# Replicated rows for the 32x32 block inverses: one transfer per block and half, and X with its chunks outside

## The chip, the cores and the metric

The kernel runs on one core of a Trainium2 chip. A core has five engines, each with its own instruction stream in a fixed order: PE (TensorE, matrix products; its weight load is listed as PEld), DVE (VectorE), ACT (ScalarE), POOL (GpSimd) and SP (SyncE), which here does nothing but issue DMA transfers. Sixteen DMA engines move the data. Engines wait for each other, and for transfers, by semaphores. The metric is the device time of one execution in microseconds (us); less is better.

## The reference, cut to what matters

Two layers over 2048 tokens of width 1024. The first is a gated DeltaNet (GDN, 8 heads), the second gated linear attention (GLA, 4 heads); each has an input projection, a mixer over chunks of tokens, a gate, an output projection and a layer norm. The change touches GDN alone, where each chunk needs a unit lower triangular system solved:

```python
kb = k * beta
A = jnp.where(strict, jnp.einsum('bhncd,bhnsd->bhncs', kb, k) * decay, 0.0)
eye = jnp.eye(CHUNK, dtype=A.dtype)
rhs = jnp.concatenate([v * beta, kb * jnp.exp(gc)[..., None]], axis=-1)
uw = lax.linalg.triangular_solve(A + eye, rhs, left_side=True, lower=True, unit_diagonal=True)
```

The kernel forms the inverse of A + eye explicitly, for chunks of 128 tokens.

## The kernel before

**Tiling.** Tokens go in 4 groups of 512, each 4 chunks (NC) of 128. A *unit* is one head of one layer in one group: 32 GDN units and 16 GLA units, 48 in all, in the order of PHASES: GDN groups 0 and 1, GLA group 0, GDN group 2, GLA 1, GDN 3, GLA 2, GLA 3. GDN units thus come as numbers 0 to 31 among themselves; "unit 12" below is head 4 of group 1. Each unit has four parts: gemms (input projections on PE, products written to PSUM tiles psg), preps (per-chunk matrices), chains (the recurrence over 4 chunks, PSUM tiles psh), outs (output projection, psc and pso).

**Weights.** Projection weights stream from HBM through 9 buffers called wc, 256 KB per load (wc<-wk), issued by SP as soon as a buffer is free; output weights (wo) come by the same queue. On their first use weights come as wraw and are split by ACT and POOL into a high and a low part, which are stored as wk.

**Inverse of the 32x32 blocks** (in gdn_prep, lines 845 to 865). D1 holds the matrix A of 4 chunks, 128x128 each. ACT copies the four diagonal 32x32 blocks into a tile X0 (named own in the code) of 128 partitions x (32 columns x 4 chunks). Two stores on ACT's queue bring it to DRAM: whole rows as blk (late in the code), the first 16 columns as blkq (early). Then SP loads the tile Arep back, in which every partition of block b holds a copy of the block's rows: rows 16 to 31 in full from blk (Arep<-blk, 1 MB), rows 0 to 15 cut to 16 columns from blkq (Arep<-blkq, 0.5 MB). The inverse X starts from the identity (a POOL copy) and is found in 31 steps, q from 31 down to 1, each two DVE operations: Xt = (row q of Arep) × (column q of X), then X −= Xt. Steps 31 to 16 read the first part of Arep, steps 15 to 1 the second. DVE then spreads X into the block-diagonal Tm, transposes it to U, and PE joins the blocks to 64 and 128.

**Layout.** X is (column j, chunk n) with the chunk innermost: a step works on q·4 adjacent elements.

**Order.** No order is written by hand. A recorder notes every operation; a planner (place) then simulates the engines with a cost per operation and a lag until its result can be read, and fixes each engine's order. For a DMA the cost is the time on SP's queue and the lag the time until it has landed. Engines run that order whatever really happens: an engine that waits holds up all that stands behind it. An Arep transfer waits on SP for its store, and the wc and wo loads stand behind it.

Of the kernel before, what the change touches and what calls it, by code (L numbers as in the profile page):

```python
# [12 lines left out]
ALU = mybir.AluOpType  # L13
# [3 lines left out]
P = 128  # L17
# [5 lines left out]
NC = TG // P  # L23
# [90 lines left out]
def size_of(shape):  # L114
    n = 1
    for k in shape[1:]:
        n *= k
    return n


class Recorder:
# [61 lines left out]
    def cost(self, op, dst, every):  # L183
        key = op.key
        n = size_of(dst.shape)
        psum = any(isinstance(a, View) and a.of.psum for a in every)
        op.func = None
        if key == "t":
            mov = size_of(every[2].shape) if op.name == "matmul" else size_of(every[1].shape)
            if op.name == "transpose":  # L190
                op.cost = 2 * dst.shape[0] / 2.4 + 4
            elif every[1].dtype == F32:
                op.cost = 2 * max(mov / 1.2 + 3, 0.85 * every[1].shape[-1] + 2)
            else:
                op.cost = mov / 2.25 + 4.5
            op.lag = 210
            op.func = op.name == "matmul" and min(dst.shape[0], every[1].shape[0]) < P
        elif key == "d":
            size = 4 * n * dst.shape[0]
            tag = dst.of.tag if isinstance(dst, View) else ""  # L200
            op.cost, op.lag = 630 if tag == "wc" or tag[:2] == "wk" else 560 if tag == "wraw" else 480, DMA_LAG + size / 170
            if tag == "Arep":
                op.cost, op.lag = 720, REP_LAG + size / 400
            elif tag in ("y", "woraw"):
                op.lag = 9500
        elif key == "a":
            size = 4 * n * dst.shape[0]
            op.cost, op.lag = 340, DMA_LAG + size / 170 + (2500 if isinstance(every[1], View) and every[1].of.tag == "xraw" else 0)
        elif key == "v":
            n = max(n, max(size_of(a.shape) for a in every))  # L210
            took = (150 if psum else 160) + 1.04 * n
            if op.name in ("tensor_reduce", "copy_predicated", "tensor_tensor_scan"):
                took += 1.0 * n
            if op.name != "tensor_tensor" and any(isinstance(a, (View, bass.AP)) and size_of(a.shape) == 1
                                                  for a in every[1:]):
                took += 62 if psum or n < 512 else 85
            op.cost, op.lag = took - 80, 80 + LAG
        elif key == "s":
            took = (165 if psum else 210) + 0.833 * n
            if any(isinstance(op.kw.get(k), (View, bass.AP)) for k in ("scale", "bias")):  # L220
                took += 100 + 67 * ("scale" in op.kw and "bias" in op.kw)
            if "accum_out" in op.kw:
                took += 190
            if op.name == "activation":
                op.func = "ln" if op.args[2] == AF.Ln else None if op.args[2] in (AF.Copy, AF.Square, AF.Identity,
                                                                                 AF.Abs) else "exp"
            op.cost, op.lag = took - 95, 95 + LAG
        else:
            took = 140 + 2.8 * n if len(every) > 2 else 185 + n
            if op.args[-1] == ALU.pow:  # L230
                took = 450 + 160 * n
            op.cost, op.lag = took - 40, 40 + LAG
# [143 lines left out]


LAG, DRAIN = 60, 35
DMA_LAG, REP_LAG, SLACK = 3500, 8500, 100
INSPECT = None  # L380


# [1 line left out]
def trunk(ctx, tc, x, xT, w_in1, conv, a_log, dt_bias, nw1, w_out1, w_in2, gk_up, gk_b, nw2, w_out2,  # L384
# [3 lines left out]
    v, s, g = (rec.engine(e, k) for e, k in ((nc.vector, "v"), (nc.scalar, "s"), (nc.gpsimd, "g")))  # L388
    pe, sync, acts = rec.engine(nc.tensor, "t"), rec.engine(nc.sync, "d"), s
# [10 lines left out]
    def T(tag, shape, bufs=1, dt=F32, p=None):  # L400
        p = p or sb
        count[0] += 1
        shape, n = list(shape), size_of(shape)
        if p is dr:
            tag = f"{tag}_{count[0]}"
        if tag not in rec.tags:
            rec.tags[tag] = [p.tile([shape[0], n], dt, tag=f"{tag}_{k}", name=f"{tag}_{k}") for k in range(bufs)]
        slots = rec.tags[tag]
        t = View(Tracked(tag, slots, p is ps, count[0], rec.rank), slots[0][:])
        if len(shape) == 3:  # L410
            t = t.rearrange("p (a b) -> p a b", a=shape[1])
        elif len(shape) == 4:
            t = t.rearrange("p (a b c) -> p a b c", a=shape[1], b=shape[2])
        return t
# [11 lines left out]
    def bc(ap, at, n):  # L426
        sh = list(ap.shape)
        return ap.unsqueeze(at).broadcast_to(sh[:at] + [n] + sh[at:])
# [3 lines left out]
    def C(k):  # L432
        return cst[:, k, :]

    ident = C(C_ID)
    id32 = T("id32", [P, 32])
# [50 lines left out]
    def small(tag, n, bufs=2):  # L487
        return T(tag, [P, n], bufs)
# [311 lines left out]
    def gdn_prep(u):  # L800
# [15 lines left out]
        ss, r, qn = small("ss", 2 * NC), small("rr", NC), small("qn", NC)  # L816
# [25 lines left out]
        A = D1  # L842
        rec.rank = R_PREP
        Tm, U, W2 = T("Tm", [P, NC, P]), T("U", [P, NC, P]), T("W2", [P, NC, P // 2])
        own = T("X0", [P, 32 * NC])
        for r0 in range(0, P, 32):
            r = slice(r0, r0 + 32)
            s.copy(own[r].rearrange("p (j n) -> p n j", n=NC), A[r, :, r])
        late, early = (T(f"{k}_{u.at}", [P, 32 // m * NC], p=dr) for m, k in ((1, "blk"), (2, "blkq")))
        acts.dma_start(late[:], own[:])  # L850
        acts.dma_start(early[:], own[:, :16 * NC])
        R = T("Arep", [P, 3 * 16 * 16 * NC])
        n = 16 * 32 * NC
        sync.dma_start(R[:, :n], bc(late[:].rearrange("(b s) n -> b (s n)", b=4)[:, n:], 1, 32))
        sync.dma_start(R[:, n:], bc(early[:].rearrange("(b s) n -> b (s n)", b=4)[:, :n // 2], 1, 32))
        X, xt = T("X", [P, 32, NC]), T("Xt", [P, 31, NC])
        g.tensor_copy(X[:], bc(id32[:], 2, NC))
        for q in range(31, 0, -1):
            at = (q - 16) * 32 * NC if q >= 16 else n + q * 16 * NC
            row = R[:, at:at + q * NC].rearrange("p (j n) -> p j n", n=NC)  # L860
            v.tensor_tensor(xt[:, :q], row, bc(X[:, q], 1, q), ALU.mult)
            v.tensor_tensor(X[:, :q], X[:, :q], xt[:, :q], ALU.subtract)
        v.tensor_tensor(Tm[:].rearrange("p n (b j) -> p n b j", j=32), bc(X[:].rearrange("p j n -> p n j"), 2, 4),
                        bc(C(C_BLK).rearrange("p (b j) -> p b j", j=32), 1, NC), ALU.mult)
        v.transpose(flat(U[:]), flat(Tm[:]))
        for half in (32, 64):
# [359 lines left out]
```

## Time and profile before

| | |
|---|---|
| median of 3 runs | 3476.01 us (3469.45 to 3477.48) |
| profiled execution | 3474.92 us |
| its span, first to last instruction | 3472.7 us |
| mean granted TensorE clock | 0.933 |
| HBM read, written | 480.36 MB, 129.30 MB |

The span cut in 40 slices, each digit the busy share of a slice in tenths (9 is 90% or more):

```profile
PE   8688876877888889997788888999599878999997
DVE  6577665775665658666576666756476666764755
DMA  5455655665444455876445444757544545576754
```

How to read what the prediction shows. A row of a group or timeline reads: line of the code (L364 is the recorder's own line for nearly all), engine, operation, out<-in by tile names with buffer numbers left out, partitions x elements and type, count. In a grouped row busy us and the mean ns of one follow, then the idle time of the engine just before them and who ended it. A list of waits has total us, times, and the longest. Rows of windows have the stretch in us, the busy time of each engine with its number of instructions, the granted clock, the busy share of the 16 DMA engines and GB/s. SPq and ACTq are the DMA issues on SP and ACT.

### The profile page before, as it was taken

Reading aid. Unit: us, or ns where it says so; the run is one execution under the profiler, and the core shown is the slowest. Engines: PE = TensorE matmul, PEld = TensorE weight load, DVE = VectorE, ACT = ScalarE, POOL = GpSimd, SP = SyncE. Lnnn points to the kernel's source line nnn. Section 1 sums busy time; section 2 is a strip of 40 time slices with the busy share of each in tenths; the row PEclk is TensorE's granted clock in tenths of the full one; section 3 lists DMA queues with packets and bytes.
Section 4 is the critical chain, followed back from the end, with each engine's and each line's share of the span. In section 5 each row is a group of like instructions: output and inputs, shape, how many; then the busy total and the mean of one; then the engine's idle time right before and its main releaser. Section 6 shows DMA issues by size and latency. Waiting matters only on the chain. (4 is left out here: it accounts for less than half of the span.)

```text
span 3472.7 us, 47799 instructions
## 1 busy us (share of the span) xinstructions
PE 2992.4 (86%) x16172; PEld 2464.3 (71%) x16172; DVE 2207.5 (64%) x5374; ACT 1263.2 (36%) x3233; POOL 506.4 (15%) x848
## 2 busy tenths in 40 slices
PE   8688876877888889997788888999599878999997
PEld 6567655756666668786677767888477766888886
DVE  6577665775665658666576666756476666764755
ACT  5344433533322335433233333433133323433431
POOL 4332332230000023311000000001000000000100
PEclk9799998998999999999999998999799999999999
DMA  5455655665444455876445444757544545576754
GB/s 178 137 163 184 200 189 163 197 219 160 135 141 135 145 162 175 273 257 218 119 142 162 146 129 164 242 190 245 170 132 138 155 140 148 170 260 221 228 185 143
DMA packets 464485, 612.84 MB, mean 176 GB/s; under 512 B 41152, under 2 KB 391616, under 8 KB 448112
## 3 DMA queue, kind: packets, MB, share of 16 engines
q1 hardware_dynamic: 445616, 589.80, 54.2%
q10 hardware_dynamic: 18624, 20.00, 1.8%
q8 instruction: 127, 2.08, 0.2%
q14 instruction: 118, 0.97, 0.1%
HBM read 480.36 MB, written 129.30 MB: 176 GB/s over the span
## 5 line engine op out<-in xcount | busy, mean ns | idle before, releaser
L364 PE MATMUL psg<-xh,wc 128*128 128x512 f32 x3936 | 1365.7, 414 | 261.2 <-DMA wc<-wk 195.5
L364 PEld LDWEIGHTS psg<-xh,wc 128*128 128x128 f32 x3936 | 753.4, 193 | 439.3 <-DMA wc<-wk 204.8
L364 PE MATMUL psg<-xl,wc 128*128 128x512 f32 x1968 | 813.1, 414 | 0.2
L364 PE MATMUL pso<-wo,oth 128*128 128x512 f32 x1472 | 500.7, 414 | 40.7 <-DVE y L364 38.9
L364 PEld LDWEIGHTS psg<-xl,wc 128*128 128x128 f32 x1968 | 380.9, 194 | 78.9 <-DVE xl L364 1.5
L364 DVE SCALAR_TENSOR_TENSOR y<-pso,z,y 128x512 f32<-128x512 f32 x368 | 274.4, 746 | 164.2 <-PE pso L364 152.5
L364 POOL TENSOR_TENSOR wc<-wraw,wc 128x256 fp32r<-128x256 f32 (+1 forms) x336 | 282.1, 858 | 571.1 <-ACT wc L364 547.4
L364 DVE TENSOR_TENSOR Xt<-Arep,X 128x124 f32<-128x124 f32 (+30 forms) x992 | 235.8, 238 | 196.9 <-DMA Arep<-blk 173.8
L364 DVE SCALAR_TENSOR_TENSOR acc<-pb,taps,acc 128x512 f32<-128x512 f32 x384 | 303.7, 793 | 84.7 <-ACT acc L364 79.4
L364 PEld LDWEIGHTS pso<-wo,oth 128*128 128x128 f32 x1472 | 267.2, 192 | 107.1 <-DVE y L364 53.3
L364 PE MATMUL pso<-wo,otl 128*128 128x512 f32 x736 | 297.9, 405 | 0.7 <-DVE otl L364 0.7
L364 PE MATMUL psg<-wc,xh 128*128 128x256 f32 (+1 forms) x1344 | 266.4, 292 | 12.0 <-DMA wc<-wk 9.4
L364 DVE TENSOR_TENSOR X<-X,Xt 128x124 f32<-128x124 f32 (+30 forms) x992 | 234.7, 237 | 23.7
L364 PEld LDWEIGHTS psg<-wc,xh 128*128 128x128 f32 x1344 | 215.6, 191 | 21.4 <-DMA wc<-wk 8.1
L364 ACT ACTIVATE th<-psg 128x512 f32<-128x512 f32 (+1 forms) x170 | 95.3, 572 | 351.7 <-PE psg L364 339.5
L364 ACT CAST wc<-wraw 128x256 fp32r<-128x256 f32 (+1 forms) x336 | 124.9, 405 | 226.2 <-DMA wraw<-in_w_in 191.0
L364 PE MATMUL psg<-wc,xl 128*128 128x256 f32 (+1 forms) x672 | 188.5, 288 | 0.0
L364 POOL TENSOR_SCALAR z<-ssq 128x4 f32<-128x4 f32 x44 | 13.1, 297 | 1095.1 <-ACT junk L364 1076.1
L364 DVE SCALAR_TENSOR_TENSOR S<-S,eg,psh 128x256 f32<-128x256 f32 x128 | 61.2, 478 | 173.2 <-PE psh L364 172.8
L364 PEld LDWEIGHTS pso<-wo,otl 128*128 128x128 f32 x736 | 140.8, 191 | 31.0 <-DVE otl L364 2.2
L364 ACT COPY pb<-psg 128x512 f32<-128x512 f32 x128 | 74.9, 585 | 222.7 <-PE psg L364 217.9
L364 POOL COPY halo<-pb 128x3 f32<-128x3 f32 x128 | 33.0, 258 | 705.2 <-ACT pb L364 703.5
(193 smaller groups left out, 4435.8 us busy)
## 6 DMA issues: line engine op xcount, KB each, us to landing
wc<-wk SPq DMA_DIRECT2D x856, 256.0 KB
wo<-wok SPq DMA_DIRECT2D x70, 1024.0 KB
wk<-wc SPq DMA_DIRECT2D x272, 256.0 KB
wraw<-in_w_in SPq DMA_DIRECT2D x336, 128.0 KB
Arep<-blk SPq DMA_DIRECT2D x32, 1024.0 KB
wok<-wo SPq DMA_DIRECT2D x24, 1024.0 KB
wc<-wk SPq DMA_DIRECT2D x80, 272.0 KB
Arep<-blkq SPq DMA_DIRECT2D x32, 512.0 KB
```

The source lines that it names most:

```text
L364: tc.keep_in_program_order(op.call(*[real(a) for a in op.args], **{k: real(a) for k, a in op.kw.items()}))
```

## The change

Three edits belong together. *Transfers:* each of the two Arep loads becomes four, one for each block b; a load copies one contiguous row to 32 partitions, so its source pattern has the repetition (32) outermost. *Layout:* X, Xt, X0 and blk have the chunk outside and the column inside, (n, j) for (j, n). A step reads and writes four runs of q elements, rows of Arep keep a fixed width of 32 or 16 columns, and blkq, which takes 16 of every 32 columns, is stored in pieces of 16 elements. *Planner:* an Arep load counts 430 ns on SP's queue instead of 720, and its lag is 7000 ns instead of 8500 plus size/400.

```diff
             if tag == "Arep":
-                op.cost, op.lag = 720, REP_LAG + size / 400
+                op.cost, op.lag = 430, REP_LAG
...
-DMA_LAG, REP_LAG, SLACK = 3500, 8500, 100
+DMA_LAG, REP_LAG, SLACK = 3500, 7000, 100
...
         for r0 in range(0, P, 32):
             r = slice(r0, r0 + 32)
-            s.copy(own[r].rearrange("p (j n) -> p n j", n=NC), A[r, :, r])
+            s.copy(own[r].rearrange("p (n j) -> p n j", n=NC), A[r, :, r])
         late, early = (T(f"{k}_{u.at}", [P, 32 // m * NC], p=dr) for m, k in ((1, "blk"), (2, "blkq")))
         acts.dma_start(late[:], own[:])
-        acts.dma_start(early[:], own[:, :16 * NC])
+        acts.dma_start(early[:].rearrange("p (n j) -> p n j", n=NC), own[:].rearrange("p (n j) -> p n j", n=NC)[:, :, :16])
         R = T("Arep", [P, 3 * 16 * 16 * NC])
         n = 16 * 32 * NC
-        sync.dma_start(R[:, :n], bc(late[:].rearrange("(b s) n -> b (s n)", b=4)[:, n:], 1, 32))
-        sync.dma_start(R[:, n:], bc(early[:].rearrange("(b s) n -> b (s n)", b=4)[:, :n // 2], 1, 32))
-        X, xt = T("X", [P, 32, NC]), T("Xt", [P, 31, NC])
-        g.tensor_copy(X[:], bc(id32[:], 2, NC))
+        for part, rows, c in ((late, slice(16, 32), slice(0, n)), (early, slice(0, 16), slice(n, 3 * n // 2))):
+            for b in range(4):
+                sync.dma_start(R[b * 32:(b + 1) * 32, c],
+                               part[b * 32 + rows.start:b * 32 + rows.stop, :].rearrange("s n -> (s n)").unsqueeze(0)
+                               .broadcast_to([32, c.stop - c.start]))
+        X, xt = T("X", [P, NC, 32]), T("Xt", [P, NC, 31])
+        g.tensor_copy(X[:], bc(id32[:], 1, NC))
         for q in range(31, 0, -1):
-            at = (q - 16) * 32 * NC if q >= 16 else n + q * 16 * NC
-            row = R[:, at:at + q * NC].rearrange("p (j n) -> p j n", n=NC)
-            v.tensor_tensor(xt[:, :q], row, bc(X[:, q], 1, q), ALU.mult)
-            v.tensor_tensor(X[:, :q], X[:, :q], xt[:, :q], ALU.subtract)
-        v.tensor_tensor(Tm[:].rearrange("p n (b j) -> p n b j", j=32), bc(X[:].rearrange("p j n -> p n j"), 2, 4),
+            w = 32 if q >= 16 else 16
+            at = (q - 16) * w * NC if q >= 16 else n + q * w * NC
+            row = R[:, at:at + w * NC].rearrange("p (n j) -> p n j", n=NC)[:, :, :q]
+            v.tensor_tensor(xt[:, :, :q], row, X[:, :, q:q + 1].broadcast_to([P, NC, q]), ALU.mult)
+            v.tensor_tensor(X[:, :, :q], X[:, :, :q], xt[:, :, :q], ALU.subtract)
+        v.tensor_tensor(Tm[:].rearrange("p n (b j) -> p n b j", j=32), bc(X[:], 2, 4),
                         bc(C(C_BLK).rearrange("p (b j) -> p b j", j=32), 1, NC), ALU.mult)
```

The planner's numbers move instructions on every engine. Two places matter below. The first is SP's queue around the Arep loads of unit 12 (names carry buffer numbers; wc_3_140 is the fourth of the nine weight buffers; the last column is the destination's shape). Before:

```order
L364 DMA wc_1_138<-wk_833_0_314 128x2x256
L364 DMA wc_2_139<-wk_837_0_315 128x2x256
L364 DMA Arep_0_206<-blk_12_2186_0_474 128x1x2048
L364 DMA Arep_0_206<-blkq_12_2187_0_475 128x1x1024
L364 DMA wc_3_140<-wk_840_0_316 128x2x256
L364 DMA wc_4_141<-wk_843_0_317 128x2x256
L364 DMA wc_5_142<-wk_846_0_318 128x2x256
L364 DMA wc_6_143<-wk_932_0_323 128x2x256
L364 DMA wc_7_144<-wk_935_0_324 128x2x256
```

And now:

```order
L364 DMA wc_3_140<-wk_840_0_316 128x2x256
L364 DMA wc_4_141<-wk_843_0_317 128x2x256
L364 DMA wc_5_142<-wk_846_0_318 128x2x256
L364 DMA wc_6_143<-wk_932_0_323 128x2x256
L364 DMA Arep_0_206<-blk_12_2186_0_474 32x2048 x4
L364 DMA Arep_0_206<-blkq_12_2187_0_475 32x1024 x4
L364 DMA wc_7_144<-wk_935_0_324 128x2x256
L364 DMA wc_8_145<-wk_938_0_325 128x2x256
L364 DMA wo_0_227<-wok_914_0_321 128x2048
```

Two Arep rows became eight, still side by side, and four weight loads (wc_3 to wc_6) that stood behind them now stand ahead. The second place is DVE at the first steps of the same unit. Before:

```order
L364 SCALAR_TENSOR_TENSOR Rt_0_219<-psh_0_218,s1_0_198,vt_0_113 128x256
L364 TENSOR_TENSOR Xt_0_208<-Arep_0_206,X_0_207 128x124
L364 SCALAR_TENSOR_TENSOR y_1_224<-pso_0_232,z_1_210,y_1_224 128x512
L364 TENSOR_TENSOR X_0_207<-X_0_207,Xt_0_208 128x124
L364 TENSOR_TENSOR Xt_0_208<-Arep_0_206,X_0_207 128x120
```

And now:

```order
L364 SCALAR_TENSOR_TENSOR y_1_224<-pso_0_232,z_1_210,y_1_224 128x512
L364 SCALAR_TENSOR_TENSOR vt_0_113<-th_1_108,psg_2_111 128x512
L364 SCALAR_TENSOR_TENSOR y_0_223<-pso_0_232,z_1_210,y_0_223 128x512
L364 TENSOR_TENSOR Xt_0_208<-Arep_0_206,X_0_207 128x124
L364 TENSOR_TENSOR X_0_207<-X_0_207,Xt_0_208 128x4x31
L364 TENSOR_TENSOR Xt_0_208<-Arep_0_206,X_0_207 128x4x30
```

Two accumulations of the previous unit's output (y_1 and y_0, which free the PSUM tile pso) moved from behind the first step to ahead of it, and a step is now four runs (4x30) where it was one (120).

## The prediction

> **What bounds the kernel now.** The page comes first: who is busy for how long.
>
> ```profile
> span 3472.7 us, 47799 instructions
> PE 2992.4 (86%) x16172; PEld 2464.3 (71%) x16172; DVE 2207.5 (64%) x5374; ACT 1263.2 (36%) x3233; POOL 506.4 (15%) x848
> ```
>
> PE, which multiplies, is idle for 3472.7 − 2992.4 = 480 us. Nothing else comes near a full load, so the question is what those 480 us wait for. The list of waits names two that belong together:
>
> ```profile
> DVE Xt L364 <- DMA Arep<-blk: 173.8, 22, 11.4
> PE psg L364 <- DMA wc<-wk: 204.9, 25, 19.9
> ```
>
> PE waits for weights (wc), 25 times, up to 19.9 us at once; DVE waits for the replicated rows (Arep). Their place in time is found by cutting the span at the 32 issues of Arep<-blk (one per GDN unit, 68.9 to 2901.1 us) and asking for the 30 us behind each, and then for everything between. Columns are PE, PEld, DVE, ACT, POOL busy, granted clock, DMA share, GB/s; the first, the unit-12 and the last of 32 rows, and the sum:
>
> ```profile
> 69.00:99.00 30.00, 12.29 (x52) 8.65 (x50) 12.96 (x16) 8.79 (x20) 7.12 (x8) 0.82 0.41 121
> ...
> 994.00:1024.00 30.00, 14.39 (x63) 11.65 (x62) 11.50 (x19) 6.59 (x17) 2.62 (x5) 0.77 0.37 99
> ...
> 2901.00:2931.00 30.00, 15.90 (x79) 12.98 (x77) 12.77 (x25) 7.50 (x19) 2.33 (x5) 0.84 0.61 142
> sum 960.00, PE 565.85 PEld 450.25 DVE 385.00 ACT 234.38 POOL 74.72; mean PE 17.68 PEld 14.07 DVE 12.03 ACT 7.32 POOL 2.33
> ```
>
> The rest of the span, 33 stretches; one inside a GDN unit, and the sum:
>
> ```profile
> 1683.00:1713.00 30.00, 30.00 (x146) 25.25 (x145) 28.41 (x99) 12.45 (x36) 2.82 (x6) 1.00 0.32 100
> ...
> sum 2513.00, PE 2426.58 PEld 2014.05 DVE 1822.48 ACT 1028.78 POOL 431.64; mean PE 73.53 PEld 61.03 DVE 55.23 ACT 31.18 POOL 13.08
> ```
>
> This is the main reading. Behind the issues PE idles 960.00 − 565.85 = **394 us**; in the other 2513 us it idles 86 us, 3.4%. Four fifths of all idle time sits in the 30 us after the Arep transfers start, 12.3 us per unit.
>
> Unit 12 shows how. SP's timeline, then PE's, then DVE's (start, length, what, idle before):
>
> ```profile
> 993.87 0.56 SPq L364 DMA_DIRECT2D Arep<-blk  x1
> 994.53 0.53 SPq L364 DMA_DIRECT2D Arep<-blkq  x1
> ```
>
> ```profile
> 995.80 17.79 SPq L364 DMA_DIRECT2D wc<-wk  x3
> ```
>
> ```profile
> 1003.87 0.82 PE L364 MATMUL psg<-cst,acc 128*128 128x128 f32 x6
> 1020.29 0.80 PE L364 MATMUL psg<-xh,wc 128*128 128x512 f32 x1 [15.61 <-DMA wc<-wk]
> ```
>
> ```profile
> 1014.45 0.29 DVE L364 TENSOR_TENSOR Xt<-Arep,X 128x124 f32<-128x124 f32 x1 [7.74 <-DMA Arep<-blk]
> ```
>
> Arep<-blk goes out at 993.87 and DVE gets it at 1014.45, 20.6 us later. The three weight loads issued behind it need 17.79 us on SP alone. The usual length of such an issue, and that of a transfer which copies one row to all partitions (Gb), as minimum/median/maximum ns:
>
> ```profile
> L364 SPq DMA_DIRECT2D wc<-wk x936: 319/518/9521, 753.4 to 3433.4; - x188
> ```
>
> ```profile
> L364 ACTq DMA_DIRECT2D Gb<-gcT x32: 326/327/397, 50.8 to 2811.9; - x32
> ```
>
> So three issues of about 0.5 us took 17.79: SP was held up. PE used the weights it had until 1004.69 (10.8 us after the Arep issue) and then stood for 15.6 us. Windows inside that stall tell what the DMA engines did:
>
> ```profile
> 1006.00:1009.00 3.00, 0.00 (x0) 0.00 (x0) 0.71 (x2) 0.00 (x0) 0.00 (x0) 1.00 0.23 66
> ...
> 1015.00:1018.00 3.00, 0.00 (x0) 0.00 (x0) 0.00 (x0) 0.00 (x0) 0.00 (x0) 0.50 0.37 130
> ```
>
> PE idle, everyone idle, and of 16 DMA engines 0.23 × 16 = 3.7 are working. **About four engines do the replication** while twelve stand still, and weights, of which each engine carries a part, cannot land until those four are through. Four is also the outermost step count of the old source pattern: four blocks b, each repeated 32 times.
>
> **The change part by part.** *The transfers.* Sizes, from the page's list of issues:
>
> ```profile
> Arep<-blk SPq DMA_DIRECT2D x32, 1024.0 KB
> ...
> Arep<-blkq SPq DMA_DIRECT2D x32, 512.0 KB
> ```
>
> That is 1536 KB, 1.573 MB, per unit. At the 66 GB/s of 1006 to 1009 it takes 24 us, which fits the 20.6 us to the first half and a stall that ends at 26. The new transfers have 32 copies of a row as their outermost step on both sides; nothing in the pattern holds them to four engines. If all 16 work at the rate those 3.7 show (66 / 3.7 = 17.8 GB/s each), it is 285 GB/s, 5.5 us per unit. The trace has that rate in another stretch:
>
> ```profile
> 741.00:776.00 35.00, 30.77 (x136) 23.32 (x136) 31.73 (x88) 13.96 (x36) 14.41 (x20) 0.97 0.88 285
> ```
>
> So the two ends are 24 us (nothing won) and 5.5 us, and I take the lower because an ordinary stretch with mixed transfers already reaches it. The decisive number is the cover, 10.8 us: anything drained by then is invisible to PE. Beside this row the Trainium skill, "DMA: Bandwidth & Descriptors", section "Why a DMA increments its semaphore by 16 and not by 1", says that a copy uses the largest number of engines up to 16 that divides the outermost non-trivial size of both sides: 4 before, 16 after. The trace agrees for before, with 3.7.
>
> *SP's issues.* Eight in place of two, 192 more in all. Two took 993.87 to about 995.15, 1.3 us. One new issue lies between Gb's 0.33 us and the old 0.56, plus under 0.1 between them: eight are 3.3 to 5.1 us, so the first weight load behind them starts 2 to 4 us later. Behind the burst stand wc and wo loads, for which PE waits. Even 5.1 us of issuing and then 5.5 us of data, if nothing overlapped, is 10.6 us, still just under the cover. In the new order four more weight loads of unit 12 stand ahead of the burst, which lengthens the cover. I take 0 us, with 4 us × 32 = 128 us if the cover is gone.
>
> *The order.* The planner now counts 8 × 0.43 us of issuing and a lag of 7.0 us. Before, it counted on about 11 us and got 20.6: its order was built for a transfer twice as fast as the real one. A burst that drains in 6 to 9 us agrees with the new numbers. Moves elsewhere I price at 0 ± 1%, ±30 us: the 3.4% outside the windows is what its orders reach where its lags hold.
>
> *DVE, ACT and the blkq store.* Rows:
>
> ```profile
> L364 DVE TENSOR_TENSOR Tm<-X,cst 128x512 f32<-128x512 f32 x32 | 34.3, 1072 | 0.7
> L364 DVE TENSOR_TENSOR qd<-kq,Gb 128x512 f32<-128x512 f32 x32 | 22.1, 690 | 0.5
> L364 DVE TENSOR_TENSOR D<-Gb 128x256 f32<-128x256 f32 x192 | 79.0, 436 | 17.3 <-PE psc L364 14.3 <-PE psh L364 2.7
> L364 DVE TENSOR_TENSOR Xt<-Arep,X 128x124 f32<-128x124 f32 (+30 forms) x992 | 235.8, 238 | 196.9 <-DMA Arep<-blk 173.8
> L364 ACT COPY X<-D 32x128 f32<-32x128 f32 x128 | 53.5, 418 | 75.6 <-DVE D L364 74.3
> ```
>
> Tm reads X in steps of 16 bytes and takes 1072 ns where an equal product takes 690; with chunks outside it reads runs, −0.38 us a unit, 12 us in all. The Xt and X steps keep 4q elements each but walk four runs of q. D<-Gb (GLA's scaled()) already walks such runs, and takes 436 ns for 256 elements, on the line of 690 for 512: no change, bounded above by Tm's penalty (0.38/512 per element × 64 elements × 62 steps = 3 us a unit). The X0 copy (418 ns) writes runs now; it can only gain, at most 4 × 0.2 us a unit. All of it lies on DVE and ACT, which the stretch 1683 to 1713 shows can be 95% busy (DVE) with PE at 30.00 of 30.00. So: nothing on PE's path. The blkq store writes 512 pieces of 64 bytes where it wrote 128 of 256; SP's list of waits shows what a store's lateness costs now:
>
> ```profile
> SPq L364 <- DMA blk<-X: 26.4, 9, 4.0
> ```
>
> At most 4.0 us, 9 times; as long again for the slower store would be 128 us on SP, under the same cover. I take 0, since the second half is first read at step 15, 16 steps behind the first.
>
> *The clock.* After each stall PE starts at half clock. The same matmul in unit 12:
>
> ```profile
> 1023.02 0.54 PE L364 MATMUL pso<-wo,otl 128*128 128x512 f32 x1
> 1023.40 0.39 PE L364 MATMUL psg<-xh,wc 128*128 128x512 f32 x1
> ```
>
> From 1020.29 to 1023.40 it runs at half: 3.1 us, 1.6 us lost. Times 32 that is **50 us** which go with the stalls.
>
> *The sum.* PE's 565.85 us in the 32 windows, at the 3.4% idle of elsewhere, leave 20 us idle: 394 − 20 = 374 us. So 3472.7 − 374 − 50 = 3049 us of span. The profiled execution took 3474.92, 2.2 more than its span: 3051, and its own time is 1.1 below the median of 3476.01. I say **3050 us**.
>
> **The rivals.** *A short stall stays.* SP's burst plus the slower store eats the cover: 3 to 4 us of idle per unit, 100 to 128 us, about 3150 to 3180. For: 10.8 us is one unit's cover, and 10.6 us the longest drain; another unit may have less. Against: in unit 12 four weight loads moved ahead. 0.10, 3160.
>
> *The eight transfers pay each for itself.* They drain in about 17 us, half the gain: (17 − 10.8) × 32 = 198 us stay, about 3250. Against: the stretch 741 to 776 moves its 285 GB/s in transfers of 256 KB and less; the commonest of its list of issues:
>
> ```profile
> wk<-wc SPq DMA_DIRECT2D x11, 256.0 KB
> ```
>
> 0.09. Here the Trainium skill, same page, section "Bandwidth", speaks against the change: transfers of at least 1 MiB are to be preferred, and the page's fixed 2.0 us each would make eight of them 19.6 us if they ran one after another, so about 3330; no run here shows such a transfer alone.
>
> *The source is the limit, and it gets slower.* If 66 GB/s comes from reading one row over and over, not from the number of engines, the 24 us stay and the extra 2 to 4 us of issuing stand before the weights: 3 × 32 = 96 us more, 3570. It decides where the new drain exceeds about 24 us. For: these are the only large transfers with a repeated source. Against: DMA share was 0.23; a starved source would show all engines busy with slow packets. 0.05, of which 0.01 for no gain or loss.
>
> **How the numbers follow.** Forecast 0.76, with its own range 2990 (no idle left in the windows, the order's 30 us to the good) to 3110 (those 30 us to the bad and 1 us of stall per unit); the short stall 0.10; half the gain 0.09; the source 0.05. The range 2990 to 3180 holds the first two. A measurement of this kernel tells 0.3%, some 10 us, from nothing. Faster 0.95, within 0.01, slower 0.04.
>
> **What would show it.** Right: PE's wait for wc<-wk falls from 204.9 to under 50 us and DVE's for Arep<-blk from 173.8 to under 40; the longest SP issue of wc falls from 9.5 to about 1 us; the windows behind the Arep issues show PE over 27 of 30 us and clock 1.00; Tm<-X,cst falls to 0.7 us. Wrong: DMA share near 0.25 in those windows (the pattern did not matter); or Arep on time and PE still idle, with DVE near 100% or waits for another engine in its place.

## The result, and the profile after

The median falls from 3475.08 (median of four runs; the 3476.01 above is of three) to **3029.24 us** (4 runs, 3024.38 to 3030.93): a ratio of 0.8717, 95% interval 0.8702 to 0.8732. The profiled execution took 3028.51 us with a span of 3026.3. The page of the changed kernel, the rows that answer to those of before:

```profile
span 3026.3 us, 48052 instructions
...
PE 2926.2 (97%) x16172; PEld 2419.0 (80%) x16172; DVE 2201.4 (73%) x5374; ACT 1243.6 (41%) x3233; POOL 499.8 (17%) x848
```

The span is 446.4 us shorter. PE's idle time went from 480.3 to 100.1 us, −380.2, and its busy time fell by 66.2 us though it does the same 16172 matmuls. Most of both lies in the 30 us behind each unit's first Arep issue (first unit, unit 12, and the sum of the 32):

```profile
68.00:98.00 30.00, 22.16 (x89) 15.75 (x87) 24.33 (x49) 16.09 (x44) 14.95 (x20) 0.94 0.56 154
...
825.00:855.00 30.00, 30.00 (x136) 24.35 (x135) 25.50 (x78) 3.60 (x7) 2.84 (x5) 1.00 0.86 249
...
sum 960.00, PE 916.84 PEld 736.60 DVE 803.57 ACT 366.71 POOL 154.76; mean PE 28.65 PEld 23.02 DVE 25.11 ACT 11.46 POOL 4.84
```

PE idles 960.00 − 916.84 = 43 us there where it idled 394, which is 351 of the 380 us, and does 916.84 us of work in them where it did 565.85. The busy time fell because PE ran less at half clock: by the clock records of the two traces it was busy at half clock for 183.0 us before and for 56.6 us now, and half of the difference is 63 us. In unit 12 it never stops, the clock stays at 1.00, and the DMA engines are 0.86 busy at 249 GB/s, against 0.37 and 99. The two waits that were read before (DVE for Arep, PE for weights), and the minimum, median and maximum of SP's weight issues:

```profile
DVE Xt L364 <- DMA Arep<-blk: 7.5, 8, 2.1
```

```profile
PE psg L364 <- DMA wc<-wk: 20.9, 14, 4.6
```

```profile
L364 SPq DMA_DIRECT2D wc<-wk x936: 319/518/1615, 624.9 to 2986.0; - x188
```

From 173.8, 204.9 and a longest issue of 9521 ns. SP's timeline around unit 12's replication, and DVE's first step:

```profile
825.46 2.12 SPq L364 DMA_DIRECT2D Arep<-blk  x4
827.69 3.39 SPq L364 DMA_DIRECT2D Arep<-blkq  x4
```

```profile
836.33 0.28 DVE L364 TENSOR_TENSOR Xt<-Arep,X 128x124 f32<-128x124 f32 x1
```

The burst holds SP for about 5.6 us, and the first step runs 10.9 us after the first issue, with no wait for Arep ahead of it (it was 20.6 us, 7.74 of them waited): DVE's order puts the y of the previous unit first. The page now has landing times for these issues, each from its own issue, median us in the last column:

```profile
Arep<-blk SPq DMA_DIRECT2D x128, 256.0 KB, 5.4
...
Arep<-blkq SPq DMA_DIRECT2D x128, 128.0 KB, 6.4
```

The small terms, as groups by form:

```profile
L364 ACT COPY X<-D 32x128 f32<-32x128 f32 x128 | 37.8, 295 | 38.5 <-DVE D L364 37.3
L364 DVE TENSOR_TENSOR Tm<-X,cst 128x512 f32<-128x512 f32 x32 | 22.0, 689 | 0.8
```

The mean of one is the number behind the busy time: Tm fell from 1072 to 689 ns and the X0 copy from 418 to 295. The Xt steps went from 238 to 241 ns on average and the X steps from 237 to 245.

### The profile page after: what moved, and what is told of

It reads as the page before. It is cut to its first block, busy times and chain, and to the rows that moved or that the text cites. A ratio compares the mean times of both kernels' runs of the same rounds, so it can differ in the third digit from the quotient of the medians.

```text
span 3026.3 us, 48052 instructions
## 1 busy us (share of the span) xinstructions
PE 2926.2 (97%) x16172; PEld 2419.0 (80%) x16172; DVE 2201.4 (73%) x5374; ACT 1243.6 (41%) x3233; POOL 499.8 (17%) x848
## 5 line engine op out<-in xcount | busy, mean ns | idle before, releaser
L364 PE MATMUL psg<-xh,wc 128*128 128x512 f32 x3936 | 1349.5, 409 | 29.0 <-DMA wc<-wk 16.3
L364 PEld LDWEIGHTS psg<-xh,wc 128*128 128x128 f32 x3936 | 740.5, 190 | 195.8 <-DMA wc<-wk 20.6
L364 PE MATMUL pso<-wo,oth 128*128 128x512 f32 x1472 | 486.1, 406 | 19.1 <-DVE y L364 17.6
L364 PEld LDWEIGHTS psg<-xl,wc 128*128 128x128 f32 x1968 | 374.4, 190 | 76.4 <-DVE xl L364 1.7
L364 DVE TENSOR_TENSOR X<-X,Xt 128x124 f32<-128x124 f32 (+30 forms) x992 | 242.6, 245 | 23.9
L364 PEld LDWEIGHTS psg<-wc,xl 128*128 128x128 f32 x672 | 126.1, 189 | 2.7
```

The costliest lines, as they stand in the source:

```text
L364: tc.keep_in_program_order(op.call(*[real(a) for a in op.args], **{k: real(a) for k, a in op.kw.items()}))
```

## The experiments

My theory was the number of DMA engines. Three rivals stood against it, so that four explanations were to be told apart: the number of DMA engines on the replication; the planner's new numbers and the order they make; transfers cut small, so that weights pass between them; and the layout with the chunks outside.

**One part at a time.** Four kernels make one part alone or undo one part.

*The planner's numbers alone*, on the kernel before:

```diff
-                op.cost, op.lag = 720, REP_LAG + size / 400
+                op.cost, op.lag = 430, REP_LAG
...
-DMA_LAG, REP_LAG, SLACK = 3500, 8500, 100
+DMA_LAG, REP_LAG, SLACK = 3500, 7000, 100
```

> The kernel before with the planner's two numbers of the change and nothing else: two transfers, old layout. If the number of DMA engines on the replication is the cause, the transfers still take 24 us and the time is that of before, 3475 us, or up to 60 us more, since the order now reckons with a lag of 7 us. If the new order is the cause, about 3030 us.

Measured 3502.96 us, ratio 1.0072 (1.0046 to 1.0097): the numbers by themselves make the kernel a little slower.

*The change with its transfers undone:*

```diff
-        for part, rows, c in ((late, slice(16, 32), slice(0, n)), (early, slice(0, 16), slice(n, 3 * n // 2))):
-            for b in range(4):
...
+        sync.dma_start(R[:, :n], bc(late[:].rearrange("(b s) n -> b (s n)", b=4)[:, n:], 1, 32))
+        sync.dma_start(R[:, n:], bc(early[:].rearrange("(b s) n -> b (s n)", b=4)[:, :n // 2], 1, 32))
```

> The change with its transfers undone: chunks outside, new numbers, but two transfers with the four blocks outermost. Engines as the cause: as in the run with the numbers alone, less at most 12 us for Tm, so 3440 to 3530 us. Layout as the cause: about 3030 us.

Measured 3493.92 us, 1.0059 (1.0035 to 1.0082). Layout and numbers together bring nothing; the time is that of the numbers alone.

*Eight transfers and the new numbers, old layout*, on the kernel before with the numbers:

```diff
-        sync.dma_start(R[:, :n], bc(late[:].rearrange("(b s) n -> b (s n)", b=4)[:, n:], 1, 32))
-        sync.dma_start(R[:, n:], bc(early[:].rearrange("(b s) n -> b (s n)", b=4)[:, :n // 2], 1, 32))
+        for part, rows, c in ((late, slice(16, 32), slice(0, n)), (early, slice(0, 16), slice(n, 3 * n // 2))):
+            for b in range(4):
...
```

> Eight transfers and the new numbers, old layout (chunks inside). It has the order of the change almost to the instruction. Engines as the cause: 3029 us, and 0 to 12 us more for Tm's and X0's strides. Layout as the cause: about 3475 us.

Measured 3034.41 us, 0.8733 (0.8712 to 0.8753). The transfers bring all of it; the layout's share cannot be told from nothing (the change itself is 0.8717, and the intervals overlap).

*The change with the planner's old numbers:*

```diff
-                op.cost, op.lag = 430, REP_LAG
+                op.cost, op.lag = 720, REP_LAG + size / 400
...
-DMA_LAG, REP_LAG, SLACK = 3500, 7000, 100
+DMA_LAG, REP_LAG, SLACK = 3500, 8500, 100
```

> The change with the planner's numbers of before (720 ns of issuing each, lag 8500 plus size/400). Engines as the cause: 3030 us within 30 us, since the transfers still land in 6 to 9 us and the planner only reckons them late. New order as the cause: well above 3100 us.

Measured 3022.98 us, 0.8702 (0.8681 to 0.8723): the same as the change. The new numbers were not needed.

**One number of engines after another.** The transfers have two properties that the old ones lacked: they are short, and their repetition stands outermost. The next four keep the eight transfers, their sizes, and the order of every engine, and write the repetition of 32 as k times 32/k, so that the source's outermost step count is k (k stands for the number that each run has):

```diff
                                part[b * 32 + rows.start:b * 32 + rows.stop, :].rearrange("s n -> (s n)").unsqueeze(0)
-                               .broadcast_to([32, c.stop - c.start]))
+                               .unsqueeze(0).broadcast_to([k, 32 // k, c.stop - c.start]))
```

> The change with each transfer's repetition of 32 written as 16 times 2. Order, number and size of transfers are those of the change. A control for the three that follow: 3029 us within 10 us by every theory that does not turn on how the pattern is written.

> The same with 8 times 4. Engines as the cause: eight of them, 1.573 MB at 8 x 17.8 GB/s is 11 us and some 2 us to start, a little over the cover of 10.8 us: a stall of 0 to 4 us per unit, 3040 to 3160 us. Small transfers (that weights slip in between eight short ones) as the cause: 3029 us.

> The same with 4 times 8: eight transfers of the change's size, each with an outermost step count of four as before. Engines as the cause: 24 us per unit again and the stall with it, 3430 to 3580 us. Small transfers as the cause: 3029 us.

> The same with 2 times 16. Engines as the cause: 1.573 MB at 2 x 17.8 GB/s is 44 us; less the cover of 10.8 us that is a stall of 33 to 38 us per unit, 4080 to 4300 us with the clock's loss. Small transfers as the cause: 3029 us.

Measured, with PE's idle time behind the issues (960 us less the sum of the 32 windows) and, from the semaphore records of each trace, the time from a unit's first Arep issue to the last landing of its eight transfers (a landing is the last write to the transfer's semaphore; median of the 32 units):

| k | time, us | ratio to before | 95% interval | idle behind the issues, us | last landing, us |
|---|---|---|---|---|---|
| 16 | 3025.12 | 0.8698 | 0.8669 to 0.8727 | 43 | 10.2 |
| 8 | 3050.30 | 0.8771 | 0.8735 to 0.8807 | 56 | 11.8 |
| 4 | 3292.38 | 0.9464 | 0.9432 to 0.9496 | 245 | 19.9 |
| 2 | 3719.68 | 1.0693 | 1.0637 to 1.0748 | 526 | 34.6 |

In the kernel before the last landing is 25.8 us behind the first issue, in the change 10.2.

The sums of the windows for 4 and for 2:

```profile
sum 960.00, PE 715.28 PEld 563.39 DVE 552.22 ACT 288.73 POOL 114.89; mean PE 22.35 PEld 17.61 DVE 17.26 ACT 9.02 POOL 3.59
```

```profile
sum 960.00, PE 434.09 PEld 336.65 DVE 350.49 ACT 200.29 POOL 57.36; mean PE 13.57 PEld 10.52 DVE 10.95 ACT 6.26 POOL 1.79
```

Nothing but the pattern's outermost count differs, and the time follows it: this is the cause. Small transfers alone would have given 3029 us four times. The number of engines can be counted. In the trace of before, the semaphore of unit 12's Arep<-blk is written once 1.0 us after the issue and then four times, 18.1 to 20.6 us after it; every Arep transfer there has one write just behind its issue and four late ones. With k = 8, 4 and 2 every transfer has one such early write and 8, 4 and 2 late ones, and with k = 16, as in the change itself, 16 writes: read as one report of each engine, that is k engines. A window of the run with k = 2, inside a stall, shows the count in the DMA share too (the column before the last):

```profile
1107.00:1110.00 3.00, 0.00 (x0) 0.00 (x0) 0.00 (x0) 0.00 (x0) 0.00 (x0) 1.00 0.13 55
```

0.13 × 16 = 2.1 engines at 55 GB/s, 26 GB/s each. The count is the one that the Trainium skill, "DMA: Bandwidth & Descriptors", section "Why a DMA increments its semaphore by 16 and not by 1", gives: the number of engines is the largest up to 16 that divides the outermost size of both sides. The trace agrees here (2.1) and before (3.7).

Two of the expectations were too high: 3430 to 3580 us for k = 4 and 4080 to 4300 for k = 2. They took 17.8 GB/s per engine from the old transfers, which makes 24 and 44 us of data; the last landings came at 19.9 and 34.6 us. From 4 to 2 engines each unit loses (3712.7 − 3289.5) / 32 = 13.2 us of span, about the 14.7 us that the landing moves.

How do late transfers stop PE? The prediction had two answers side by side: SP was held up at its issues, and weights could not land while the four engines were busy. SP's weight issues with k = 4:

```profile
L364 SPq DMA_DIRECT2D wc<-wk x936: 319/518/1662, 699.1 to 3251.2; - x188
```

No weight issue is held up (1.7 us at the longest, as in the changed kernel), and PE still loses 245 us. So the stall does not need SP to be stuck. But weights are only one of its ways. In the stall with k = 2 from above, PE did not wait for weights:

```profile
1117.85 1.22 PE L364 MATMUL pso<-wo,oth 128*128 128x512 f32 x2 [12.07 <-DVE y L364]
```

```profile
1115.26 0.29 DVE L364 TENSOR_TENSOR Xt<-Arep,X 128x124 f32<-128x124 f32 x1 [12.39 <-DMA Arep<-blk]
```

DVE stood for the late Arep at the first step, in its fixed order, and the y that frees PE's tile pso stands behind that step. The prediction did not price this way. It was there before, too: of PE's 480.3 us of idle time 204.9 ended with weights (wc), 152.9 with DVE and 104.0 with ACT; now it is 20.9, 43.7 and 16.3.

**Four engines, three ways.** Four engines gave 3494 us as two transfers and 3292 as eight. Order, arrangement of the blocks, or length of the transfers? The first run gives the two transfers the order of the change, through the planner's cost:

```diff
-                op.cost, op.lag = 430, REP_LAG
+                op.cost, op.lag = 4 * 430, REP_LAG
```

> The two transfers of before in the new layout, with the planner told that each costs SP four times 430 ns: that gives the order of the change almost to the instruction, which the eight transfers on 4 engines had too (3292 us). If the old order made the 200 us between those and the two transfers (3494 us), about 3290 us. If the replication itself is slower when four engines carry four different blocks at once (the stretch behind the issues is some 5 us longer per unit there), 3430 to 3480 us.

Measured 3479.32 us, 1.0022 (1.0003 to 1.0040), with 960.00 − 529.81 = 430 us idle behind the issues:

```profile
sum 960.00, PE 529.81 PEld 414.72 DVE 403.69 ACT 230.14 POOL 81.62; mean PE 16.56 PEld 12.96 DVE 12.62 ACT 7.19 POOL 2.55
```

The order is not it: 187 us remain between the two. The second run makes eight transfers again, each with all four blocks and four of the sixteen rows:

```diff
+        for part, r0, c0, w in ((late, 16, 0, 32 * NC), (early, 0, n, 16 * NC)):
+            for i in range(4):
+                sync.dma_start(R[:, c0 + i * 4 * w:c0 + (i + 1) * 4 * w],
+                               bc(part[:].rearrange("(b s) n -> b (s n)", b=4)[:, (r0 + i * 4) * w:(r0 + i * 4 + 4) * w], 1, 32))
```

> Eight transfers per unit of the change's sizes in its order and layout, but each carries four of the sixteen rows for all four blocks (outermost step count four, one block to each of four engines) and not all sixteen for one block. Against the eight transfers with 4 times 8 (four engines, all on one block, 3292 us) and the two paced transfers (four engines, four blocks, 3479 us), all in the same order. If four engines are slower on four blocks at once than on one, 3430 to 3510 us. If two long transfers are slower than eight short ones, about 3290 us.

Measured 3299.77 us, 0.9478 (0.9452 to 0.9503). Four blocks on four engines are not slower in themselves, so the paced run met the second branch of its expectation by its number, not by its reason. The landings say where the two transfers lose (medians of the 32 units): their first, 1024 KB in pieces of 8 KB, lands 20.4 us after its issue, while the four that replace it have landed at 14.1 in both runs with eight. The second, 512 KB in pieces of 4 KB, takes 5.2 us more; its four replacements take 5.7 (k = 4) and 6.2 (four blocks). So length alone is not it, or the 512 KB would be slow as well. Slow are 8 KB pieces of four blocks at once in a transfer of 1 MB; 8 KB pieces of one block and 2 KB pieces of four blocks are not. Which of these properties does it stays open.

**Two long transfers on sixteen engines.** Here the Trainium skill (same page, section "Bandwidth") asks for transfers of at least 1 MiB (its table there is of transfers issued by GpSimd; these are issued by SP). The rows are stored four times over, so that two transfers per unit have an outermost count of 16:

```diff
-        acts.dma_start(late[:], own[:])
+        for i in range(4):
+            acts.dma_start(late[:].rearrange("(b c s) w -> c b s w", b=4, c=4)[i], own[:])
...
+        sync.dma_start(R[:, :n], bc(late[:].rearrange("(x s) n -> x (s n)", x=16)[:, n:], 1, 8))
+        sync.dma_start(R[:, n:], bc(early[:].rearrange("(x s) n -> x (s n)", x=16)[:, :n // 2], 1, 8))
```

> The change with two transfers per unit that have an outermost step count of 16: the rows are stored four times over (eight small stores on ACT's queue in place of two), and each transfer copies 16 stored blocks 8 times each. Engines as the cause: 3029 us within 30 us, since sixteen engines carry it again. Many short transfers as the cause: above 3290 us.

Measured 3092.37 us, 0.8911 (0.8888 to 0.8934): most of the gain is there with long transfers, so shortness is not needed for it, but it misses the expected 30 us by 33. The transfers are not to blame: the last landing comes 10.0 us behind the first issue (median of the 32 units), in the change 10.2. Behind the issues PE idles 960.00 − 902.72 = 57 us, 14 more than in the change; the rest of the loss lies elsewhere. One wait that the change hardly has stands out:

```profile
PE psh L364 <- ACT wt L364: 19.3, 17, 4.5
```

ACT copies wt and also issues the six extra stores per unit. The stores themselves became slow: their outermost count is four, each reports from four engines, and they land after 3.5 us (blk) and 4.6 us (blkq), median, where the change's two land after 1.8 and 2.7. That the stores cost the 63 us is argued, not shown, since the order moved too. The 1 MiB made no difference to the replication here: with 16 engines, 1024 and 512 KB or 256 and 128 KB, it lands after 10 us.

**Another queue.** The kernel before with its two transfers issued by ACT:

```diff
-        sync.dma_start(R[:, :n], bc(late[:].rearrange("(b s) n -> b (s n)", b=4)[:, n:], 1, 32))
-        sync.dma_start(R[:, n:], bc(early[:].rearrange("(b s) n -> b (s n)", b=4)[:, :n // 2], 1, 32))
+        acts.dma_start(R[:, :n], bc(late[:].rearrange("(b s) n -> b (s n)", b=4)[:, n:], 1, 32))
+        acts.dma_start(R[:, n:], bc(early[:].rearrange("(b s) n -> b (s n)", b=4)[:, :n // 2], 1, 32))
```

> The kernel before with its two transfers issued on ACT's queue in place of SP's. If weights wait because they stand behind the replication in one queue, they now pass beside it: the stall shrinks to a few us per unit, 3050 to 3250 us. If four engines full of replication hold any weight load up, whatever the queue, the stall stays: 3400 to 3550 us, ACT's own wait for the store included.

Measured 3468.45 us, 0.9973 (0.9952 to 0.9995). The two waits in this run:

```profile
DVE Xt L364 <- DMA Arep<-blk: 239.9, 24, 14.3
PE psg L364 <- DMA wc<-wk: 119.5, 35, 11.7
```

PE waits less for weights than before (204.9, longest 19.9), and DVE more for the replicated rows (173.8); PE's waits for DVE rise from 152.9 to 224.0 us and eat up what the weights gained. A second queue does not help where the engines behind it are the same four.

## Why the prediction was right

*What bounds the kernel, and the four engines.* Right, and shown: DMA share 0.23 was read as four engines held by the outermost count of the source; the semaphore records of before show four reports per transfer, and the runs from k = 16 to 2 change that count alone. The way from there to PE was right in part: the prediction let weights alone carry the delay, and only 204.9 of the 480.3 us end with them, as shown above. It did no harm to the number, since the sum took all idle time behind the issues, whatever ended it.

*The transfers' price.* Right in its sum. Predicted were 3.3 to 5.1 us of issuing and 5.5 us of data, 10.6 us at most; the median unit has 3.9 us of issuing and its last landing 10.2 us after the first issue. Unit 12 is longer, 5.6 and 13.2 us, without harm. The rate under it, 17.8 GB/s per engine, is that of the old 1 MB transfers alone: two engines showed 26 in the new ones. It did not matter for the change, but it made the expectations for 4 and 2 engines too long.

*The cover.* The idea held, its number was that of the old order. 10.8 us was measured there in unit 12; in the change's order, with slow transfers (k = 2, and the two paced ones), PE runs on for 13.9 us behind the issue in that unit. The forecast that the order lengthens the cover was right, and 13.2 us lie within it. Over all units, 32 × (last landing − 10.8 us) makes 32 us for 8 engines, 291 for 4, 480 for before and 762 for 2; measured above the change were 21, 263, 446 and 690. The short stall that was a rival did not come, nor did the other two: PE is busy for 28.65 of the 30 us on average, and five units of 32 stay under 27.

*The sum.* Predicted 374 us less idle time, 380 found; predicted 50 us from the clock, 66 found, with a mean granted clock of 0.988 for 0.933. The clock's term was under-sized: it was taken from one unit (1.6 us) and multiplied by 32. By the clock records the windows behind the issues gave (119.0 − 23.8) / 2 = 48 us, as predicted, and the rest of the span, where stalls also end, 16 more. Within the idle time two errors cancel, which is luck: 43 us stayed behind the issues, not 20, and 57 us elsewhere, not 86. The new order is not what made the 29 us elsewhere: with the planner's old numbers the same transfers leave 65 us there. So some 21 of the 29 came with the transfers alone; that they are the ends of stalls that outlast the 30 us is likely, not shown. Together: 3049 us of span predicted, 3026.3 found. The lower end of the forecast's own range, 2990, is 10 us below what its two terms give (3050 − 20 − 30 = 3000); nothing hangs on it.

*The order.* Priced at 0 ± 30 us, and right: the numbers alone on the old transfers cost 0.7%, and the old numbers on the new transfers change nothing that can be told.

*DVE, ACT, the store.* Tm's −0.38 us a unit came as predicted (1072 to 689 ns), hidden as predicted: with the old layout, Tm at its old pattern, the time is the same within the intervals. The blkq store lands 2.7 us after its issue, and as late with the old layout, whose store has whole rows. SP's wait for blk<-X is 33.7 us where it was 26.4, at most 9.6 us where it was 4.0; the run with the old layout has 32.8 and 9.5, so the small pieces are not the reason, and its time is the same.

## What to carry to other kernels

When PE waits, look at the DMA share inside the wait. Here a share of 2/16 or 4/16 while everything stood meant that one transfer ran on few engines. Not every stall shows it: in unit 12 of the paced run, where PE waited through DVE, the share was 0.79 to 0.96. Write the pattern so that the outermost step count on both sides is a multiple of 16, by splitting a transfer where its outermost dimension is small. A first estimate of what such a transfer costs is its landing time less the cover that the work in hand gives, per unit; here it came out some 10% too high where the cost was large. Half the engines cost 25 us and a quarter of them 267. And ask what else stands behind the late transfer in a fixed order: here more of PE's idle time ended with DVE and ACT than with the weights.

## What was not expected of the hardware

Four engines do the same copies faster in eight transfers than in two, 3292 and 3300 us against 3479 in the same order. A stretch in which only such copies run shows 26 GB/s per engine in the new transfers (two engines, 55 GB/s) and 17.8 in the old ones (3.7 engines, 66 GB/s), both while pieces of 8 KB move; the pieces of 4 KB show no such difference. The cause is open. And a DMA issue on SP can itself take 9.5 us, not 0.5. That is not a matter of long transfers: in the run with k = 2, with eight short ones, a weight issue took up to 10.5 us and an Arep issue up to 11.1; in that with k = 4 it was at most 1.7 and 1.3. The stall comes without it as well.
